# Moving a hybrid layer's SBUF buffers by 64 and 128 bytes

## The chip, the cores and the metric

The kernel runs on one core of a Trainium2 chip. The metric is the time of one execution on the device, in microseconds (us). All data are float32 in HBM; the result is float32.

## What is computed

One decoder layer over 256 tokens with 2048 features. The input is normed and goes through one combined projection of 12304 columns; its parts feed a gated DeltaNet branch (8 heads of 128, short convolution, delta rule) and a causal attention branch (8 heads of 128). Each branch is widened to 2048, the two are merged with sigmoid gates, projected once more, normed and added to the input:

```python
h = rms_norm(x, pre_norm_w)                     # x: 256 x 2048
proj = h @ w_in                                 # w_in: 2048 x 12304
qkv = silu(causal_depthwise_conv(proj[:, :3072], conv_w))
oa = gated_delta_rule(l2_normalize(q), l2_normalize(k), v, beta, g)
oa = oa * rsqrt(mean(oa * oa) + eps) * gdn_norm_w * silu(gdn_z)
u_a = oa @ w_branch_a                           # 1024 x 2048
ob = moba_attention(q_b, k_b, v_b) * silu(moba_z)
u_b = ob @ w_branch_b                           # 1024 x 2048
merged = sigmoid(gate_a) * u_a + sigmoid(gate_b) * u_b
out = x + rms_norm(merged @ w_out, post_norm_w) # w_out: 2048 x 2048
```

With 256 tokens there is one attention block, so the attention is plain causal attention.

## The kernel before

**Split weights.** Every float32 weight tile is taken apart in `split` (L260): `hi` is the weight rounded to float32r (a copy on ScalarE, L265), `lo` the rest (a subtraction on VectorE, L266). The input and the branch results are held the same way, as a rounded half and a rest. A product is three float32r matmuls: rounded by hi, rounded by lo, rest by hi. All of them are recorded by the helper `mm` (L176), transposes by `tr` (L179), in the order in which the program names them.

**Projections.** `proj_n` (L419) makes a chunk of 512 output columns: for each of 16 slices of 128 features it loads rows of w_in into a raw tile (pool `wraw`, three buffers, on the SyncE queue, L424), splits it in two (pool `wspl`, three buffers of hi and lo), and runs 12 matmuls per split: two slices, two halves of the tokens, three products. The moving operand is hi or lo with 512 columns (348, 348 and 344 for the three chunks of zg), the stationary one a 128 by 128 piece of the normed input, tile hT. A chunk of 512 columns is 96 matmuls. In `proj_t` (L397: the DeltaNet's q and k) it is the other way round: the weight is stationary and hT moves, with 512 and 256 columns.

**The normed input.** hT is an object of class `Halves` (L63) over two tiles, hT_0 for slices 0 to 7 and hT_1 for slices 8 to 15, so that the first half of a chunk's matmuls reads the one and the second half the other.

**Branches and output.** `seven` (L990) multiplies blocks of the branch and output weights with seven block products in place of eight (names ua, ub, y). Some operands are sums of blocks: of the weights in tiles z0, z1, z2, and of the input in four pairs of tiles, three of them in tt, tw, tv of the pool `big` and the fourth in tag s of the pool `wk` (`sum_tiles`). `product` (L964) runs 6 or 12 matmuls for a split. While the branch blocks run, chunks of the gates ga and gb run beside them (`gate_beside`, L1066).

**Every fourth split.** When the first branch block begins, `branch_pair` (L1031) closes the pool `wf` and opens a pool `wx` with one buffer in its room; from then on every fourth split takes its hi and lo from `wx` and the others from `wspl` (L262).

**Where buffers lie.** Tiles lie in SBUF pool by pool: cst, big, wraw, wspl, wk, then wf or wx; within a pool in the order of first allocation, at steps of 32 bytes per partition. Most tiles are multiples of 256 bytes per partition long. Counted from a multiple of 256 bytes, the tiles of big, wraw and wspl lie at 0, the s tiles of wk at 64, wf and wx at 192.

**Two small rows.** nrow (L193) holds the norm's weight as 16 rows of 128, loaded on the ScalarE queue and read by a transpose at the start. grs (L485, in `decays`) holds the decays of the DeltaNet, 16 rows of 128, copied from PSUM and written to DRAM at once by the GpSimd queue (L488). Each has a place of 512 bytes in cst.

Of the kernel before, what the change touches and what calls it, by code (L numbers as in the profile page):

```python
# [8 lines left out]
F32 = mybir.dt.float32  # L9
F32R = mybir.dt.float32r  # L10
# [5 lines left out]
P = 128  # L16
EPS = 1e-6
NEG = -1e30

WARM = 2  # L20
WARM2 = 1
# [84 lines left out]
def hybrid_layer(  # L106
# [16 lines left out]
    B, S, D = x.shape  # L123
    NT = S // P
    KT = D // P
# [16 lines left out]

    cst = ctx.enter_context(tc.tile_pool(name="cst", bufs=1))
    big = ctx.enter_context(tc.tile_pool(name="big", bufs=1))
    wraw = ctx.enter_context(tc.tile_pool(name="wraw", bufs=3))
    wspl = ctx.enter_context(tc.tile_pool(name="wspl", bufs=3))
    wk = ctx.enter_context(tc.tile_pool(name="wk", bufs=2))
    dram = ctx.enter_context(tc.tile_pool(name="dram", bufs=1, space=bass.MemoryType.DRAM))

    early = ExitStack()  # L150
    wf = early.enter_context(tc.tile_pool(name="wf", bufs=8))
    acc = ctx.enter_context(tc.tile_pool(name="acc", bufs=4, space=bass.MemoryType.PSUM))
# [5 lines left out]
    def aux_tile(name):  # L158
        return aux.tile([P, 512], F32, tag="aux", name=name)
# [15 lines left out]
    def mm(*args, **kwargs):  # L175
        return pin(nc.tensor.matmul(*args, **kwargs))  # L176

    def tr(*args):
        return pin(nc.tensor.transpose(*args))  # L179
# [4 lines left out]
    nba = 2 * H  # L184
# [1 line left out]
    ZG = (0, 348, 696, GW + nba)  # L186
    ZW, ZBA = ZG[3] - ZG[2], GW - ZG[2]

    nrow = cst.tile([KT, P], F32, name="nrow")
    rawk = [big.tile([P, KT // 2, 512], F32, tag=f"g{i}", name=f"rawf_k{i}") for i in range(2)]  # L190
    ones = cst.tile([P, P], F32, name="ones")
    nc.vector.memset(ones, 1.0)
# [14 lines left out]
    for c in range(KT // 2):  # L207
# [24 lines left out]
    nc.gpsimd.affine_select(  # L232
        out=mask_t, in_=mask_t, compare_op=ALU.is_ge, fill=NEG, base=0, pattern=[[1, P]], channel_multiplier=-1
    )
# [10 lines left out]
        compare_op=ALU.is_ge,  # L245
        fill=NEG,
        base=0,
# [19 lines left out]
        return hi, lo  # L267

    ncol = cst.tile([P, KT], F32, name="ncol")
    hT = Halves(*(big.tile([P, KT // 2, 2 * S], F32R, tag=f"hT{i}", name=f"hT_{i}") for i in range(2)))  # L270
    ssx = cst.tile([P, NT, 4], F32, name="ssx")

    def turn(c):
# [176 lines left out]
    def decays():  # L450

        pbt = [pt[:, ZBA:ZW] for pt in pzg]
        zz = cst.tile([P, NT, H], F32, name="zz")
        sp = cst.tile([P, NT, H], F32, name="sp")
        for t in range(NT):
            pa_ = pbt[t][:, H:]
            pin(nc.vector.scalar_tensor_tensor(zz[:, t, :], pa_, rstd[:, t : t + 1], dtb, op0=ALU.mult, op1=ALU.add))
        for t in range(NT):
            pb_ = pbt[t][:, :H]
            pin(nc.scalar.activation(beta[:, t, :], pb_, AF.Exp, scale=nrstd[:, t : t + 1]))  # L460
        pin(nc.scalar.activation(sp, zz, AF.Abs))
        pin(nc.scalar.activation(sp, sp, AF.Exp, scale=-1.0))
        pin(nc.scalar.activation(na, na, AF.Exp))
        pin(nc.scalar.activation(sp, sp, AF.Ln, bias=ones[:, 0:1]))
        pin(nc.vector.scalar_tensor_tensor(sp, zz, 0.0, sp, op0=ALU.max, op1=ALU.add))
        pin(
            nc.vector.scalar_tensor_tensor(
                sp, sp, -1.0, na.unsqueeze(1).to_broadcast([P, NT, H]), op0=ALU.mult, op1=ALU.mult
            )
        )  # L470
        nc.vector.tensor_scalar_add(beta, beta, 1.0)
        nc.vector.reciprocal(beta, beta)
        yield 0.5
        for f in late:
            f()
        yield PG_WAIT
        pg = aux_tile("pg")
        mm(pg[:, 0:nba], tri_u, sp, start=True, stop=True)
        mm(pg[:, nba : nba + H], ones, sp[:, 0, :], start=True, stop=True)
        nc.vector.tensor_copy(gcol, pg[:, 0:nba].rearrange("p (t h) -> p t h", t=NT))  # L480
        nc.vector.tensor_tensor(gx, pg[:, nba : nba + H], gcol[:, 0, :], op=ALU.subtract)
        yield PGT_WAIT
        pgt = aux_tile("pgt")
        tr(pgt[0:nba, :P], gcol.rearrange("p t h -> p (t h)"), ident)
        grs = cst.tile([nba, P], F32, name="grs")  # L485
        nc.vector.tensor_copy(grs, pgt[0:nba, :P])
        g_d = dram.tile([nba, P], F32, name="g_d")
        nc.gpsimd.dma_start(g_d, grs)  # L488
        grow = big.tile([P, NT, H, P], F32, tag="z0", name="grow")
        nc.gpsimd.dma_start(  # L490
            grow.rearrange("p t h n -> p (t h n)"),
            g_d.rearrange("a n -> (a n)").unsqueeze(0).broadcast_to([P, nba * P]),
        )
        yield D_WAIT
        for h in range(0, H, 2):
            for h_ in (h, h + 1):
                for t in range(NT):
                    pin(
                        nc.vector.scalar_tensor_tensor(
                            dec[:, h_, 2 * t * P : (2 * t + 1) * P],  # L500
                            grow[:, t, h_, :],
                            gcol[:, t, h_ : h_ + 1],
                            mask_t,
                            op0=ALU.subtract,
                            op1=ALU.add,
                        )
                    )
            pin(
                nc.vector.tensor_tensor(
                    dec[:, h : h + 2, P : 2 * P],  # L510
                    grow[:, 1, h : h + 2, :],
                    gx[:, h : h + 2].unsqueeze(2).to_broadcast([P, 2, P]),
                    op=ALU.add,
                )
            )
            yield 1


        one = wk.tile([P, 2], F32, tag="mx", name="one")
        pin(nc.vector.memset(one, 1.0))  # L520
        identity.append(big.tile([P, 16, 64], F32, tag="tv", name="tv"))
        for g in range(4):
            gp = slice(32 * g, 32 * g + 32)
            nc.gpsimd.affine_select(
                out=identity[0][gp],
                in_=one[gp, 0:1].unsqueeze(2).to_broadcast([32, 16, 64]),
                compare_op=ALU.is_equal,
                fill=0.0,
                base=g,
                pattern=[[4, 16], [-1, 64]],  # L530
                channel_multiplier=0,
            )
        for h in range(0, H, 2):
            pin(nc.scalar.activation(dec[:, h : h + 2, :], dec[:, h : h + 2, :], AF.Exp))
            if h + 2 < H:
                yield 1
        decaying.pop()
# [877 lines left out]
    pzg = proj_n(w_in, CZ + ZG[2], hT, KT, "zg2", ZW, aux_tile)  # L1415
    late.append(lambda: silu_out("zg", ZG[2], GW, pzg))
    gq.add(decays())
    for m in range(4):
        conv_silu(kTs[m // 2][m % 2], H + m, late)
# [306 lines left out]
```

## Time and profile before

| | us |
|---|---|
| median of 3 runs | 747.8 |
| lowest and highest | 747.5, 748.63 |
| span of the profiled execution | 745.7 |
| TensorE busy (matmuls) | 736.9 |
| VectorE busy | 606.8 |
| ScalarE busy | 456.2 |
| GpSimd busy | 90.8 |
| HBM traffic | 187.49 MB, mean 251 GB/s |

The span goes from the first to the last instruction of one execution; the time of a run also holds what lies around them. PE stands for TensorE's matmuls, PEld for its weight loads, DVE for VectorE, ACT for ScalarE, POOL for GpSimd, SP for SyncE. Matmuls are pipelined: the next one starts while the one before still drains, so that a matmul's duration is longer than the time from its start to the next one's start.

### The profile page before, as it was taken

To read this page: it belongs to the slowest core of one execution; us is meant where nothing else is said; L and a number is where in the kernel's file an instruction comes from. 1 tells how busy PE (TensorE), PEld (TensorE's weight loads), DVE (VectorE), ACT (ScalarE), POOL (GpSimd) and SP (SyncE) were. 2 spreads that over 40 slices of the span, in tenths; PEclk is the share of its full clock that TensorE was granted. 3 is DMA by queue.
4 is the path that set the end of the run, shared out by engine and by line. 5 is a ranking of instruction groups with operands and counts; after the bars stand their busy time and mean duration, and the time that the engine had idled before them with its cause. 6 is when DMAs were issued, how large, how long until landed. Compare 5 with 4: busy or idle time off the path is not lost.

```text
span 745.7 us, 9927 instructions
## 1 busy us (share of the span) xinstructions
PE 736.9 (99%) x3594; PEld 621.2 (83%) x3594; DVE 606.8 (81%) x957; ACT 456.2 (61%) x692; POOL 90.8 (12%) x124
## 2 busy tenths in 40 slices
PE   9999999999999999999999999999999999999995
PEld 7898988898888888888888888788888888888885
DVE  6877779997896998987556889688796799988864
ACT  6777655556775665547556766557546654765751
POOL 1000301113110101232011050010000101110000
PEclk9999999999999999999999999999999999999999
DMA  9576586548766767998478799788988889998862
GB/s 317 177 242 227 164 237 203 173 143 271 258 226 226 254 215 260 302 303 300 140 228 307 256 294 307 209 320 244 352 228 301 236 300 276 383 328 228 270 238 113
DMA packets 94199, 187.49 MB, mean 251 GB/s; under 512 B 4421, under 2 KB 25606, under 8 KB 93638
## 3 DMA queue, kind: packets, MB, share of 16 engines
q1 hardware_dynamic: 76806, 134.83, 53.9%
q0 software_dynamic: 15584, 47.20, 21.9%
q10 hardware_dynamic: 1760, 4.83, 1.8%
q8 instruction: 28, 0.46, 0.2%
q14 instruction: 21, 0.17, 0.1%
HBM read 173.20 MB, written 13.64 MB: 251 GB/s over the span
## 4 chain that ended last, share of the span: by engine, by line
PE 98%; DMA 0%; DVE 0%; DVEq 0%; issue 0%; ACTq 0%; ACT 0%
PE a_ga L176 12%; PE a_gb L176 12%; PE a_y L176 9%; PE a_ub L176 7%; PE a_zg L176 6%; PE a_k L176 6%; PE a_q L176 6%; PE a_mq L176 6%; PE a_mv L176 6%; PE a_mk L176 6%; PE a_v L176 6%; PE a_zm L176 6%; PE a_ua L176 5%; PE s L176 1%; PE po L176 1%; PE so L176 1%
## 5 line engine op out<-in xcount | busy, mean ns | idle before, releaser
L176 PE MATMUL a_ga<-hi_ga,hT 128*128 128x512 f32 x256 | 81.7, 393 | 0.0
L176 PE MATMUL a_gb<-hi_gb,hT 128*128 128x512 f32 x256 | 80.9, 391 | 0.0
L176 PEld LDWEIGHTS a_gb<-hi_gb,hT 128*128 128x128 f32 x256 | 48.0, 188 | 10.6
L176 PEld LDWEIGHTS a_ga<-hi_ga,hT 128*128 128x128 f32 x256 | 48.1, 188 | 10.1
L265 ACT CAST hi_gb<-raw_gb 128x1024 fp32r<-128x1024 f32 x32 | 33.5, 1052 | 28.1 <-PE a_gb L176 15.2
L266 DVE TENSOR_TENSOR lo_ga<-raw_ga,hi_ga 128x1024 fp32r<-128x1024 f32 x32 | 38.9, 1218 | 14.3 <-ACT hi_ga L265 14.1
L176 PE MATMUL a_ga<-lo_ga,hT 128*128 128x512 f32 x128 | 50.0, 391 | 0.0
L176 PE MATMUL a_gb<-lo_gb,hT 128*128 128x512 f32 x128 | 50.0, 391 | 0.0
L176 PE MATMUL a_zg<-hi_zg,hT 128*128 128x348 f32 (+1 forms) x192 | 46.7, 322 | 0.0
L265 ACT CAST hi_ga<-raw_ga 128x1024 fp32r<-128x1024 f32 x32 | 33.4, 1049 | 20.4 <-PE a_ga L176 16.8
L266 DVE TENSOR_TENSOR lo_gb<-raw_gb,hi_gb 128x1024 fp32r<-128x1024 f32 x32 | 38.7, 1216 | 7.3 <-ACT hi_gb L265 7.0
L176 PE MATMUL a_mv<-hi_mv,hT 128*128 128x512 f32 x128 | 41.5, 395 | 0.0
L176 PE MATMUL a_mk<-hi_mk,hT 128*128 128x512 f32 x128 | 40.5, 393 | 0.0
L176 PE MATMUL a_q<-hT,hi_q 128*128 128x512 f32 x128 | 40.2, 395 | 0.0
L176 PE MATMUL a_mq<-hi_mq,hT 128*128 128x512 f32 x128 | 39.7, 389 | 0.0
L176 PE MATMUL a_v<-hi_v,hT 128*128 128x512 f32 x128 | 39.7, 389 | 0.0
L176 PE MATMUL a_zm<-hi_zm,hT 128*128 128x512 f32 x128 | 39.7, 389 | 0.0
L176 PE MATMUL a_k<-hT,hi_k 128*128 128x512 f32 (+1 forms) x129 | 38.2, 397 | 0.0
L176 PEld LDWEIGHTS a_zg<-hi_zg,hT 128*128 128x128 f32 x192 | 33.5, 188 | 0.1
L266 DVE TENSOR_TENSOR lo_mv<-raw_mv,hi_mv 128x1024 fp32r<-128x1024 f32 x16 | 19.4, 1218 | 17.2 <-ACT hi_mv L265 16.0
L176 PE MATMUL a_zg<-lo_zg,hT 128*128 128x348 f32 (+1 forms) x96 | 30.9, 322 | 0.0
L265 ACT CAST hi_zg<-raw_zg 128x696 fp32r<-128x696 f32 (+1 forms) x24 | 18.5, 771 | 19.7 <-PE a_zg L176 7.4
(479 smaller groups left out, 2025.2 us busy)
## 6 DMA issues: line engine op xcount, KB each, us to landing
raw_ga<-in_w_in_dram SPq DMA_DIRECT2D x16, 1024.0 KB, 6.0
raw_gb<-in_w_in_dram SPq DMA_DIRECT2D x16, 1024.0 KB, 7.0
raw_y<-in_w_out_dram SPq DMA_DIRECT2D x14, 1024.0 KB, 7.8
raw_q<-in_w_in_dram SPq DMA_DIRECT2D x8, 1024.0 KB, 5.5
raw_mv<-in_w_in_dram SPq DMA_DIRECT2D x8, 1024.0 KB, 5.0
raw_v<-in_w_in_dram SPq DMA_DIRECT2D x8, 1024.0 KB, 5.0
raw_zm<-in_w_in_dram SPq DMA_DIRECT2D x8, 1024.0 KB, 5.2
raw_mq<-in_w_in_dram SPq DMA_DIRECT2D x8, 1024.0 KB, 6.4
```

The lines of the kernel that those rows point to most:

```text
L176: return pin(nc.tensor.matmul(*args, **kwargs))
L265: nc.scalar.copy(hi, raw)
L266: nc.vector.tensor_tensor(lo, raw, hi.bitcast(F32), op=ALU.subtract)
```

## The change

Three small tiles that nothing reads or writes are added. pad_w (16 floats, 64 bytes per partition) lies in front of wraw, pad_h (64 bytes) between hT_0 and hT_1, and pad_x (64 bytes) in front of the pool wf, in whose room wx is opened later. nrow and grs share one place (tag rows), which takes 512 bytes out of cst. Counted from a multiple of 256 bytes: hT_0 and the tiles allocated with it (g0, g1, ga, u1) stay at 0; hT_1 and what is allocated behind it (z0, z1, z2, tv, tt, tw) lie at 64; wraw and wspl at 128; the s tiles of wk at 192; wf and wx at 128. The instructions stay the same.

```diff
--- before.py
+++ after.py
@@ -16,6 +16,8 @@
 P = 128
 EPS = 1e-6
 NEG = -1e30
+
+PAD_H, PAD_W, PAD_X = 16, 16, 16
 
 WARM = 2
 WARM2 = 1
@@ -142,11 +144,13 @@
 
     cst = ctx.enter_context(tc.tile_pool(name="cst", bufs=1))
     big = ctx.enter_context(tc.tile_pool(name="big", bufs=1))
+    ctx.enter_context(tc.tile_pool(name="pad_w", bufs=1)).tile([P, PAD_W], F32, name="pad_w")
     wraw = ctx.enter_context(tc.tile_pool(name="wraw", bufs=3))
     wspl = ctx.enter_context(tc.tile_pool(name="wspl", bufs=3))
     wk = ctx.enter_context(tc.tile_pool(name="wk", bufs=2))
     dram = ctx.enter_context(tc.tile_pool(name="dram", bufs=1, space=bass.MemoryType.DRAM))
 
+    ctx.enter_context(tc.tile_pool(name="pad_x", bufs=1)).tile([P, PAD_X], F32, name="pad_x")
     early = ExitStack()
     wf = early.enter_context(tc.tile_pool(name="wf", bufs=8))
     acc = ctx.enter_context(tc.tile_pool(name="acc", bufs=4, space=bass.MemoryType.PSUM))
@@ -186,7 +190,7 @@
     ZG = (0, 348, 696, GW + nba)
     ZW, ZBA = ZG[3] - ZG[2], GW - ZG[2]
 
-    nrow = cst.tile([KT, P], F32, name="nrow")
+    nrow = cst.tile([KT, P], F32, tag="rows", name="nrow")
     rawk = [big.tile([P, KT // 2, 512], F32, tag=f"g{i}", name=f"rawf_k{i}") for i in range(2)]
     ones = cst.tile([P, P], F32, name="ones")
     nc.vector.memset(ones, 1.0)
@@ -267,7 +271,9 @@
         return hi, lo
 
     ncol = cst.tile([P, KT], F32, name="ncol")
-    hT = Halves(*(big.tile([P, KT // 2, 2 * S], F32R, tag=f"hT{i}", name=f"hT_{i}") for i in range(2)))
+    hT0 = big.tile([P, KT // 2, 2 * S], F32R, tag="hT0", name="hT_0")
+    big.tile([P, PAD_H], F32, name="pad_h")
+    hT = Halves(hT0, big.tile([P, KT // 2, 2 * S], F32R, tag="hT1", name="hT_1"))
     ssx = cst.tile([P, NT, 4], F32, name="ssx")
 
     def turn(c):
@@ -482,7 +488,7 @@
         yield PGT_WAIT
         pgt = aux_tile("pgt")
         tr(pgt[0:nba, :P], gcol.rearrange("p t h -> p (t h)"), ident)
-        grs = cst.tile([nba, P], F32, name="grs")
+        grs = cst.tile([nba, P], F32, tag="rows", name="grs")
         nc.vector.tensor_copy(grs, pgt[0:nba, :P])
         g_d = dram.tile([nba, P], F32, name="g_d")
         nc.gpsimd.dma_start(g_d, grs)
```

## Rows read from the trace of the kernel before

**Rows 1.** The page: span, busy time and share of each engine.

```profile
span 745.7 us, 9927 instructions
PE 736.9 (99%) x3594; PEld 621.2 (83%) x3594; DVE 606.8 (81%) x957; ACT 456.2 (61%) x692; POOL 90.8 (12%) x124
```

**Rows 2.** The page, part 4: the chain that ended last, by engine.

```profile
PE 98%; DMA 0%; DVE 0%; DVEq 0%; issue 0%; ACTq 0%; ACT 0%
```

**Rows 3.** The chain in order of time: start us, length us, engine and tile.

```profile
110.39 11.15 PE a_k L176 x64
...
176.57 21.80 PE a_v L176 x96
198.37 21.76 PE a_zm L176 x96
...
547.45 21.96 PE a_gb L176 x96
```

**Rows 4.** Windows: us; PE, PEld, DVE, ACT, POOL busy; PEclk; DMA; GB/s.

```profile
176.50:198.30 21.80, 21.80 (x98) 18.02 (x97) 15.00 (x27) 15.75 (x31) 5.07 (x8) 1.00 0.83 262
...
621.70:643.60 21.90, 21.90 (x98) 17.94 (x97) 21.90 (x28) 12.21 (x15) 2.79 (x3) 1.00 1.03 316
```

**Rows 5.** Timeline of PE in gb: start us, us, operation (out<-moving,stationary).

```profile
552.98 0.39 PE L176 MATMUL a_gb<-lo_gb,hT 128*128 128x512 f32 x1
...
555.70 0.39 PE L176 MATMUL a_gb<-lo_gb,hT 128*128 128x512 f32 x1
...
558.49 0.40 PE L176 MATMUL a_gb<-lo_gb,hT 128*128 128x512 f32 x1
...
561.24 0.39 PE L176 MATMUL a_gb<-lo_gb,hT 128*128 128x512 f32 x1
```

**Rows 6.** Timeline of PE around the fourth sums of ua.

```profile
494.97 0.39 PE L176 MATMUL a_ua<-hi_ua0p,oas_hi 128*128 128x512 f32 x1
...
497.77 0.40 PE L176 MATMUL a_ga<-hi_ga,hT 128*128 128x512 f32 x1
...
536.27 0.40 PE L176 MATMUL a_ua<-hi_ua2p,oas_hi 128*128 128x512 f32 x1
...
537.67 0.39 PE L176 MATMUL a_ua<-hi_ua2p,oas_hi 128*128 128x512 f32 x1
...
539.05 0.39 PE L176 MATMUL a_gb<-hi_gb,hT 128*128 128x512 f32 x1
```

**Rows 7.** Timeline of PE in zg, with 344 and 348 columns.

```profile
38.78 0.32 PE L176 MATMUL a_zg<-lo_zg,hT 128*128 128x344 f32 x1
...
39.73 0.32 PE L176 MATMUL a_zg<-lo_zg,hT 128*128 128x344 f32 x1
...
40.68 0.32 PE L176 MATMUL a_zg<-lo_zg,hT 128*128 128x344 f32 x1
...
85.62 0.32 PE L176 MATMUL a_zg<-lo_zg,hT 128*128 128x348 f32 x1
...
86.58 0.32 PE L176 MATMUL a_zg<-lo_zg,hT 128*128 128x348 f32 x1
...
87.54 0.32 PE L176 MATMUL a_zg<-lo_zg,hT 128*128 128x348 f32 x1
```

**Rows 8.** DMA issues: KB each, median us from issue to landing.

```profile
raw_v<-in_w_in_dram SPq DMA_DIRECT2D x8, 1024.0 KB, 5.0
...
raw_zg<-in_w_in_dram SPq DMA_DIRECT2D x8, 696.0 KB, 4.3
```

**Rows 9.** Tiles nrow and grs: min/median/max ns, first and last start us.

```profile
L179 PE MATMUL pnc<-ident,nrow x1: 256/256/256, 4.2 to 4.2; 16*128 16x16 f32 x1
...
L486 DVE COPY grs<-pgt x1: 273/273/273, 64.1 to 64.1; 16x128 f32<-16x128 f32 x1
```

## The prediction, made before the change was run

> **What bounds the kernel now.** I read the page first. Its span is 745.7 us and the matmul engine is busy in 99% of it, VectorE in 81%, ScalarE in 61% [rows 1]; the chain of work that ended last is 98% TensorE [rows 2]. So the kernel is as long as its matmul stream, and a change that only moves buffers can act on the time in two ways: through the time from one matmul's start to the next one's (below: the pitch), or through something off the stream that gets late enough to stop it. The profiled execution spans 745.7 us and the runs have a median of 747.8: 2.1 us lie around the first and the last instruction, and I add them back unchanged.
>
> The chain in order of time gives the pitch: 96 matmuls of 512 columns for zm in 21.76 us are 226.7 ns each; v has 227.1; a gb chunk of the later part has 21.96 us, 228.8 each [rows 3]. 512 columns at 2.4 GHz (granted clock 1.00, the upper level, [rows 4]) are 213.3 ns, so each matmul pays 13.4 ns, or 6%, on top of its columns. That margin is what the change can touch. The mean duration in the lists of groups (389 to 397 ns) is no help: matmuls overlap, and only starts count.
>
> **Where the addresses show already.** The change speaks of places modulo 256 bytes, and the kernel before holds several of them, so the trace prices some. From the sizes of the tiles, wspl, hT and nearly all of "big" start at 0; wx, which takes every fourth split after the first branch block, at 192; the s tiles of wk (the fourth sum of each seven-product block) at 64. I write a pair as (moving, stationary).
> - (0, 0) and (192, 0): in gb the lo matmuls that open three splits in a row stand at 552.98, 555.70, 558.49 and 561.24 [rows 5]. Twelve matmuls from wspl take 2.72 us (226.7 each), the twelve from wx 2.79 (232.5 with the edge matmul), the next twelve from wspl 2.75. So a wx split costs some 6.6 ns more per matmul, and the stream needs about 0.02 to 0.03 us to find its pace again.
> - (0, 64): twelve matmuls on the fourth sum take 2.80 us, 233.3 each; a second such block six in 1.40 [rows 6].
> - (192, 64), 128 apart: the six behind it take 1.38 us, 230 each [rows 6].
> - 348 and 344 columns: in zg the second k of each split begins 1392 or 1376 bytes later, at 112 or 96. Six matmuls at 0 and six at 112 both take 0.96 us; six at 0 and six at 96 both 0.95 [rows 7].
>
> The settled paces are 160.0, 226.7 and 233.3 ns: 24, 34 and 35 times 6.67 ns. A relation therefore costs a whole step or nothing, once the stream has settled; values between (230) stand only in short stretches.
>
> **The change part by part.** PAD_H moves hT's second half and all of "big" allotted behind it (z0 to z2, tv, tt, tw) to 64; PAD_W with it puts wraw and wspl at 128; PAD_X puts wx at 128 as well. No instruction is added or removed. (a) *Matmuls with split weights as moving operand.* The 18 chunks of v, zm, mq, mk, mv, ga, gb have 96 each, 1728; by the code the seven-product blocks and the rest of ua, ub and y have about 684. Some 1308 of these become (128, 0), some 1044 (128, 64), and 60 (the fourth sums) (128, 192). No row has either of the first two. Bounds from the nearest rows: 233.3, the price of (192, 0) and (0, 64), so +6.6 ns; below, one step less than now, 220.0, since nothing in the rows excludes a gain and 213.3 would still fit under it. I take 226.7, because the rows nearest to 128 are 96 and 112, they are long and regular, and they cost what 0 costs; the row that is 128 apart (230) has six matmuls, right behind a disturbance. (b) *wx.* 32 splits go through it, 15 with 12 matmuls and 17 with six: 282. At 226.7 each saves 6.6 ns, 1.9 us, and the 32 recoveries at 0.02 us save 0.6. Sum of (a) and (b): -2.5 us; bounds of (b) alone: -2.5 and 0. (c) *The fourth sums* keep their distance (0 to 64 becomes 128 to 192): 60 matmuls, 0, with 60 x 6.7 = 0.4 us either way. (d) *q and k*: hT is the moving operand there, 64 matmuls with 24,576 columns take 11.15 us [rows 3], 14.2 ns above the columns each. They become (0, 128) and (64, 128); about 510 matmuls by 3 ns either way are 1.5 us; I take 0. (e) *zg's 288*: bounded by a step of 6.7 ns on each either way, 1.9 us; I take 0. (f) *Loads into moved places.* raw_zg lands rows of 1392 bytes at odd places: 696 KB in 4.3 us against 1024 KB in 5.0 for raw_v [rows 8], a rate 21% lower at worst. wraw has three buffers of 5.4 us of matmuls each, so a load of 7 us that became 9 would still land inside the two buffers ahead of it; I take 0, and the cover is thin only where the DMA engines are full (rival 4). (g) *The shared row.* grs is written at 64.1 us and waits from now on for the last reader of nrow, which ran at 4.2 us [rows 9]: nothing is queued by it, cost 0.
>
> Sum: 745.7 - 2.5 + 2.1 = 745.3 us.
>
> **A rule against it.** The rows show that the same matmul with the same data sizes takes 226.7 or 233.3 ns with only the buffer's place changed [rows 5]. The Trainium skill, "SBUF — State Buffer", section "SBUF: two separate sides", holds that on the engine side only the port pair shared by VectorE and GpSimd contends and that TensorE waits for no one; by it the places of buffers could not matter and the time would stay 747.8. The trace disagrees with it, by those 6.6 ns. The page "TensorE: Matmul & The Clock Gate" of the Trainium skill, section "Wait — 56ns, not 53.3ns?", puts a warm pitch at the columns plus 2.5 ns, 215.8; this trace has nowhere such a pitch on 512 columns, and an estimate from that page's figure, 2352 x 10.9 ns, would be 26 us off.
>
> **The rivals.** (1) *The new relations cost a step or half of one*: slower. For: both long stretches away from (0, 0) pay it [rows 5, 6], and the one 128 apart pays half. Against: 96 and 112 pay nothing [rows 7]. Price: half a step (3.3 ns) on 2070 matmuls is +6.8, less 0.9 for wx and 0.6 for recoveries: 753.1. One of the two halves at a full step: between 752 and 754 as well. Both halves: 2070 x 6.67 = +13.8, 761.6. It decides as soon as more than some 380 of the matmuls pay a step. (2) *The new relations save a step* (220.0 ns): for one of the halves -7.0 or -8.7 besides the 2.5, about 737; for both -15.7 - 1.9 - 0.6, 729.6. Against: no pace under 226.7 is in the trace, and in the gb chunk of 621.7 VectorE is busy in all of the stretch and the DMA engines too [rows 4], so part of the gain would be given back there as waits for lo or raw. (3) *Places do not matter as such*, and what I read as places belongs to the order of buffers: 747.8. Against: 32 splits of wx alike, and the s tiles in other products. (4) *Loads get slower*: if rows at 64 or 128 cost 5% where DMA is full (the last 200 us), 2% to 4% of these show, 752 to 756.
>
> **How the numbers follow.** My forecast (places cost as now, wx gains): 0.34, 743.8 to 747.5 on its own. Rival 1: 0.33. Rival 2: 0.20. Rival 3: 0.08. Rival 4: 0.05. A measurement of this kernel can tell about 0.2%, 1.5 us, from no change. Faster takes 0.30 of the forecast and all of rival 2; within 0.2% takes 0.04 of the forecast and rival 3; slower the rest. Cases of both signs hold most of the chance, so the range of 8 in 10 runs from 732 (one half saving a step, or most of both) to 758 (more than one half paying one); outside lie the full gain and the full loss.
>
> **What would show it.** Right: zm's chunk still 21.76 us, gb's chunk 21.8 in place of 21.96, and no difference between every fourth split and the others. Rival 1 shows as 22.1 to 22.4 us for zm, in one half of the chunk or in both (the halves are the first and last 48 matmuls); rival 2 as 21.1; rival 4 as waits of TensorE for hi or raw with an unchanged pitch. The forecast is wrong if 128 or 64 bytes do not lie on the same flat as 96 and 112.

## The result, and the profile after

The changed kernel takes 754.0 us (median of 4 runs, 753.82 to 756.01) against 747.7 before: 1.009 times the time before, 95% interval 1.0076 to 1.0104. It is slower by 6.3 us; the forecast was 745.3, faster. The range of 732 to 758 holds 754.0, but only because it held cases of both signs.

The page of the kernel after, first its span and the busy time of each engine, then the chain that ended last by engine:

```profile
span 752.3 us, 9927 instructions
PE 743.5 (99%) x3594; PEld 621.6 (83%) x3594; DVE 607.1 (81%) x957; ACT 456.5 (61%) x692; POOL 90.5 (12%) x124
...
PE 99%; DVE 0%; ACT 0%; DVEq 0%; issue 0%
```

The same number of instructions, the same busy time within 0.4 us on every other engine, and 6.6 us more on TensorE, which is also what the span grew by [rows 1, 2]. Nothing new waits. So the loss is in the time from one matmul's start to the next one's, the pitch. The clock is not the cause: in the chunk of v the granted clock is 1.00, the upper level, with the DMA engines busy for 0.84 of the time, as in the same chunk before (1.00 and 0.83 [rows 4]). Window of the kernel after (us; PE, PEld, DVE, ACT, POOL busy; PEclk; DMA; GB/s):

```profile
176.60:198.74 22.14, 22.14 (x98) 18.07 (x97) 15.29 (x27) 15.84 (x31) 5.06 (x8) 1.00 0.84 259
```

The chain in order of time of the kernel after (start us, length us, engine and tile, count):

```profile
110.44 11.13 PE a_k L180 x64
...
176.60 22.13 PE a_v L180 x96
198.74 22.16 PE a_zm L180 x96
...
512.95 5.60 PE a_gb L180 x24
...
524.05 5.60 PE a_gb L180 x24
...
535.19 5.49 PE a_gb L180 x24
...
543.48 5.59 PE a_gb L180 x24
...
551.87 22.19 PE a_gb L180 x96
```

A chunk of v, zm or gb is 0.2 to 0.4 us longer than before, the group of k is 0.02 us shorter [rows 3]. Timeline of PE in the chunk of zm after (start us, us, operation), with three of its matmuls that have lo as moving operand; every third matmul is one:

```profile
198.81 0.40 PE L180 MATMUL a_zm<-lo_zm,hT 128*128 128x512 f32 x1
...
209.97 0.39 PE L180 MATMUL a_zm<-lo_zm,hT 128*128 128x512 f32 x1
...
219.58 0.39 PE L180 MATMUL a_zm<-lo_zm,hT 128*128 128x512 f32 x1
```

From the first to the second are the 48 matmuls on hT_0: 11.16 us, 232.5 ns each. From the second to the third are 42 on hT_1: 9.61 us, 228.8 each. Before, it was 226.7 in both halves. Worked out from all start times of the two traces and the places that the program gives the tiles (pitches over 275 ns, which hold waits, left out, and for fewer columns those as far above the time of the columns; a pair is moving, stationary):

| matmuls | before | after | change |
|---|---|---|---|
| 512 columns, wspl, first half | (0,0) 227.5 ns | (128,0) 232.7 | 1112 x 5.2 = +5.8 us |
| 512 columns, wspl, second half | (0,0) 227.3 | (128,64) 229.4 | 918 x 2.1 = +1.9 |
| 512 columns, wx, first half | (192,0) 233.3 | (128,0) 232.9 | 150 x -0.4 = -0.1 |
| 512 columns, wx, second half | (192,0) 233.3 | (128,64) 229.9 | 120 x -3.4 = -0.4 |
| fourth sums | (0,64) 233.2 | (128,192) 233.3 | 0 |
| zg, 344 and 348 columns | 159.0 | 158.3 | 288 x -0.7 = -0.2 |
| q and k, 512 and 256 columns | 174.6 | 174.4 | 510 x -0.2 = -0.1 |

Sum: +6.9 us, against 6.6 in the span.

### The profile page after: what moved, and what is told of

Its sections match the earlier page's. It is cut to its first block, busy times and chain, and to the rows that moved or that the text cites. A ratio compares the mean times of both kernels' runs of the same rounds, so it can differ in the third digit from the quotient of the medians.

```text
span 752.3 us, 9927 instructions
## 1 busy us (share of the span) xinstructions
PE 743.5 (99%) x3594; PEld 621.6 (83%) x3594; DVE 607.1 (81%) x957; ACT 456.5 (61%) x692; POOL 90.5 (12%) x124
## 4 chain that ended last, share of the span: by engine, by line
PE 99%; DVE 0%; ACT 0%; DVEq 0%; issue 0%
PE a_gb L180 12%; PE a_ga L180 12%; PE a_y L180 9%; PE a_ub L180 7%; PE a_k L180 6%; PE a_zg L180 6%; PE a_mv L180 6%; PE a_q L180 6%; PE a_mq L180 6%; PE a_mk L180 6%; PE a_zm L180 6%; PE a_v L180 6%; PE a_ua L180 5%; PE s L180 1%; PE po L180 1%; PE so L180 1%
```

## The experiments

Theory 1: the pair of places sets the pitch, by the prices above. Its rivals: the distance of the two places alone (theory 2), the load of the SBUF by DMA and the other engines (theory 3), slower loads into moved places.

**The grid of places.** The layer is replaced by cells of 36 matmuls, each cell with its own pair of places:

```python
mh, ml = hi[:, r % 2, m // 4 : m // 4 + w], lo[:, r % 2, m // 4 : m // 4 + w]
for t in range(2):
    sh = st[:, k, s // 4 + 128 * t : s // 4 + 128 * t + 128]
    sl = st[:, k, s // 4 + 256 + 128 * t : s // 4 + 256 + 128 * t + 128]
    matmul(pts[t][:, :w], sh, mh); matmul(pts[t][:, :w], sh, ml); matmul(pts[t][:, :w], sl, mh)
```

> This kernel leaves the layer out. It holds 64 cells, each 36 float32r matmuls of 512 columns in the order of a chunk (rounded by hi, rounded by lo, rest by hi, for two halves of the tokens), with the moving operand at one of eight places modulo 256 (0 to 224 in steps of 32) and the stationary one at one of eight; nothing else runs beside them. Every cell comes twice, in two orders. Theory 1 (the pair of places sets the pitch): the cells repeat what the traces of the two kernels show, (0,0) 227 ns, (192,0) and (0,64) 233, (128,0) 232.5, (128,64) 229.5, and both visits of a cell agree within 1 ns. Theory 2 (only the distance of the two places counts): all cells of one distance are alike, so (64,64) and (128,128) take 227 as (0,0) does. Theory 3 (not the places but the load of the SBUF by the other engines and the DMA): all cells take the same, 227 or less.

Timeline of PE in the grid: for each of five cells two starts that are 12 matmuls apart. In order: (0,0), (0,64), (64,64), (128,0), (128,128):

```profile
14.38 0.39 PE L45 MATMUL a<-hi,st 128*128 128x512 f32 x1
...
17.10 0.39 PE L45 MATMUL a<-hi,st 128*128 128x512 f32 x1
...
31.02 0.40 PE L45 MATMUL a<-hi,st 128*128 128x512 f32 x1
...
33.82 0.40 PE L45 MATMUL a<-hi,st 128*128 128x512 f32 x1
...
164.62 0.39 PE L45 MATMUL a<-hi,st 128*128 128x512 f32 x1
...
167.34 0.39 PE L45 MATMUL a<-hi,st 128*128 128x512 f32 x1
...
281.64 0.40 PE L45 MATMUL a<-hi,st 128*128 128x512 f32 x1
...
284.44 0.39 PE L45 MATMUL a<-hi,st 128*128 128x512 f32 x1
...
314.98 0.39 PE L45 MATMUL a<-hi,st 128*128 128x512 f32 x1
...
317.70 0.39 PE L45 MATMUL a<-hi,st 128*128 128x512 f32 x1
```

2.72 us where the two places are equal, be it 0, 64 or 128, and 2.80 at (0,64) and (128,0). All 128 visits by distance (moving minus stationary place, modulo 256; mean pitch behind the first 12 matmuls of a visit, 16 visits of eight cells each):

| distance | 0 | 32 | 64 | 96 | 128 | 160 | 192 | 224 |
|---|---|---|---|---|---|---|---|---|
| mean ns | 226.7 | 233.3 | 228.8 | 233.2 | 232.7 | 234.2 | 233.4 | 233.3 |
| lowest | 226.7 | 233.3 | 228.7 | 233.1 | 232.3 | 234.1 | 233.3 | 233.3 |
| highest | 226.7 | 233.3 | 229.0 | 233.5 | 232.8 | 234.3 | 233.5 | 233.4 |

Theory 2 holds, and theory 1 with it, since a pair fixes its distance: the cells of a distance agree within 0.5 ns, whatever the two places are. The changed kernel's halves have the distances 128 and 64, and their pitches are the grid's (232.7 and 228.8). Theory 3 falls, since the pitches are there while no other engine works and the granted clock is 1.00; the page of the grid, over its whole span:

```profile
DMA packets 612, 4.78 MB, mean 4 GB/s; under 512 B 64, under 2 KB 64, under 8 KB 64
```

What may lie behind the distance shows in the timeline of PE and its weight loads (PEld) in the grid:

```profile
299.97 0.39 PE L46 MATMUL a<-lo,st 128*128 128x512 f32 x1
299.97 0.19 PEld L47 LDWEIGHTS a<-hi,st 128*128 128x128 f32 x1
300.20 0.39 PE L47 MATMUL a<-hi,st 128*128 128x512 f32 x1
```

The weights of the next matmul (line 47) are loaded for 0.19 us from the moment at which the matmul of line 46 begins to stream its columns. Both read the SBUF at once; that the distance counts for this reason is not shown by it.

**wx at 0 alone.** The kernel before with the pad in front of wf and no other:

```diff
-PAD_H, PAD_W, PAD_X = 16, 16, 16
+PAD_H, PAD_W, PAD_X = 0, 0, 16
...
```

> The kernel before with a pad of 64 bytes in front of the pool wf alone (and the shared row): wx lies at 0, everything else as before. Theory 1 (pairs of places, prices of the two traces): 270 matmuls of wx fall from 233.3 to 227.4, so 1.6 us less than before: 746.1. Theory 3 (the load of other engines sets the pitch, wx is slow because it has one buffer): 747.7, as before.

Measured: 745.33 us, 0.9973 of before (0.9963 to 0.9983). The kernel before took 747.39 in the runs beside it. Chain of this kernel:

```profile
198.40 21.76 PE a_zm L179 x96
...
547.71 21.76 PE a_gb L179 x96
```

Timeline of PE in that chunk of gb, four starts with 12 matmuls from each to the next:

```profile
551.85 0.39 PE L179 MATMUL a_gb<-lo_gb,hT 128*128 128x512 f32 x1
...
554.57 0.39 PE L179 MATMUL a_gb<-lo_gb,hT 128*128 128x512 f32 x1
...
557.29 0.39 PE L179 MATMUL a_gb<-lo_gb,hT 128*128 128x512 f32 x1
...
560.01 0.39 PE L179 MATMUL a_gb<-lo_gb,hT 128*128 128x512 f32 x1
```

2.72 three times: every fourth split is as fast as the others now, where it took 2.79 before [rows 5], and gb is at 21.76 in place of 21.96 [rows 3]. The 2.1 us gained are step (b) of the prediction (2.5) by itself; the expectation of 1.6 had left the recoveries out.

**The two halves of the change apart.** First the weights at 128 and the whole input at 0, then the weights at 0 and hT_1 at 64:

```diff
-PAD_H, PAD_W, PAD_X = 16, 16, 16
+PAD_H, PAD_W, PAD_X = 0, 32, 16
...
-    big.tile([P, PAD_H], F32, name="pad_h")
```

> The changed kernel without the pad inside the input: hT and all of big at 0, wraw, wspl and wx at 128. Theory 1: every matmul with split weights is (128,0), 232.7 in place of 227.4 on about 2050 of them, 10.9 us more than before: 758.4, slower than the changed kernel, whose second half had (128,64). Rival (the second half is cheap for another reason than the place of hT_1): 754, as the changed kernel. Rival (the loss is in the loads into moved places): 754 too, with an unchanged pitch.

```diff
-PAD_H, PAD_W, PAD_X = 16, 16, 16
+PAD_H, PAD_W, PAD_X = 16, 48, 16
```

> The changed kernel with the weights put back: hT_1 and what is allocated behind it at 64, wraw, wspl and wx at 0. Theory 1: the first half of each chunk is (0,0) at 227.4, the second (0,64) at 233.2 on some 920 matmuls, 5.3 us more; wx gains 0.9 in its first half: 752.2. Rival (64 for the second half is good by itself, as it looks in the changed kernel, where that half is the cheaper one): 746 or less.

Measured: 757.07 us (1.0128 of before, 1.0113 to 1.0144) and 751.55 (1.0054, 1.0042 to 1.0067). Chain of the first:

```profile
199.19 22.31 PE a_zm L180 x96
...
554.40 22.31 PE a_gb L180 x96
```

And of the second:

```profile
198.77 22.11 PE a_zm L180 x96
...
551.25 22.08 PE a_gb L180 x96
```

22.31 us are 232.4 ns for all 96 matmuls: without the pad inside the input the second half pays as the first, and the kernel is slower still. 22.11 are 230.3, the mean of 227 and 233.4: with the weights at 0 the same pad costs, since it turns the second half's distance from 0 into 192. So 64 bytes under hT_1 are neither good nor bad by themselves, as theories 1 and 2 have it and the rival did not.

**Finer distances, and whose weights.** As the grid, with distances in steps of 4 bytes, and with two pairs in turn:

```python
for a, o in ((hi, 0), (lo, 0), (hi, 256)):
    m, s = places[j % len(places)]
    j += 1
    f = s // 4 + o + 128 * t
    matmul(pts[t][:, :w], st[:, k, f : f + 128], a[:, r % 2, m // 4 : m // 4 + w])
```

> This kernel leaves the layer out and measures the pitch of 512-column matmuls alone, as the grid of places did, now with distances (moving minus stationary place) from -32 to 96 bytes in steps of 4, and 128, 256, 512, 768 and 1024; and cells in which two pairs of places alternate from one matmul to the next. Theory A (the distance modulo 256 counts, on a grid of 32 bytes or finer): 256, 512, 768 and 1024 take 226.7 as 0 does, and between 0 and 32 the pitch goes from 226.6 to 233.4 at one point or in steps; a distance that takes 220 is possible at a place that the grid of 32 left out, I give it one chance in five. Theory B (the distance modulo 512 or more): 256 takes 230 or more. For the alternating pairs: if a matmul is slowed by the load of the weights of the next one while its own columns stream, then (0,0),(128,128) is slow (232.8) and (0,128),(128,0) fast (226.7); if its own pair counts, the other way round.

Timeline of PE, two starts that are 12 matmuls apart in each of three cells: distance 4; the pairs (0,128),(128,0) in turn; the pairs (0,0),(128,128) in turn:

```profile
79.81 0.40 PE L49 MATMUL a<-lo,st 128*128 128x512 f32 x1
...
82.64 0.40 PE L49 MATMUL a<-lo,st 128*128 128x512 f32 x1
...
182.65 0.39 PE L49 MATMUL a<-lo,st 128*128 128x512 f32 x1
...
185.41 0.39 PE L49 MATMUL a<-lo,st 128*128 128x512 f32 x1
...
296.70 0.40 PE L49 MATMUL a<-lo,st 128*128 128x512 f32 x1
...
299.54 0.40 PE L49 MATMUL a<-lo,st 128*128 128x512 f32 x1
```

Four bytes cost 10 ns (236.7). Distances of 256, 512, 768 and 1024 take 226.7, so 256 bytes are the period; 226.7 came also at -4, 28 and 60, up to 240 at -12, 20 and 68, and nothing below 226.7 anywhere: the chance of one in five that I gave to 220 did not come true. The pairs in turn: with each matmul's own pair equal and the next weights 128 away, 2.84 us, 236.7 ns; the other way round 2.76, 230.0. That fits next weights that count for more than the matmul's own, as the overlap in the timeline suggests. It is not settled: the second one is not down at 226.7, and the first is above the 232.7 of a cell in which both are 128 away, so the two do not simply add up.

**Other widths.** The same loop with the stationary operand at 0 and other numbers of columns:

> As the grid of places, the layer left out: the stationary operand at 0, the moving one at places 0 to 240, with 256, 320, 344, 348, 384, 448, 480 and 496 columns. Theory A (the start of the moving operand counts): place 0 is the fastest at every width. Theory B (what counts is the place that the stream of columns has reached when the next weights are loaded, so the width comes in too): the fastest place shifts with the width; it is 0 at 256, 320, 384 and 448 columns (whole multiples of 256 bytes) and lies elsewhere at 344, 348, 480 and 496, and at 344 and 348 the places 0, 96 and 112 are all slow or all middling, which is why the rows with 344 and 348 columns before the change showed no difference.

Timeline of PE, cells with 348 columns and the moving operand at 144, at 112 and at 0, two starts 12 matmuls apart in each:

```profile
136.10 0.32 PE L49 MATMUL a<-lo,st 128*128 128x348 f32 x1
...
137.94 0.32 PE L49 MATMUL a<-lo,st 128*128 128x348 f32 x1
...
194.62 0.32 PE L49 MATMUL a<-lo,st 128*128 128x348 f32 x1
...
196.54 0.32 PE L49 MATMUL a<-lo,st 128*128 128x348 f32 x1
...
356.92 0.32 PE L49 MATMUL a<-lo,st 128*128 128x348 f32 x1
...
358.82 0.32 PE L49 MATMUL a<-lo,st 128*128 128x348 f32 x1
```

153.3 ns at 144, 160.0 at 112, 158.3 at 0. With 348 columns the good place is 144 (16 came to the same pace on one of its two visits), and 0 and 112 are both bad. With 512 columns 0 is good. The place that is cheapest moves with the width, as theory B says, but not by the rule that it gave: at 256 columns 0 and 96 are the dearest (120.0), and 192 has the cheapest visit (113.3) but 117.8 on its other one; at 448, 64 and 160 (200.0) beat 0 (202.7); at 320 all eight places take 146.7. At 344 columns no place has 153.3 on both visits: 0 and 112 settled there once and at 157.7 and 159.8 the other time, and 96 took 157.5.

**q and k.** The same with two matmuls of 512 columns on hi and two of 256 on lo:

> As the grid of places, the layer left out, in the order of q and k: two matmuls of 512 columns with hi stationary, two of 256 with lo; the moving operand at 0, hi at eight places and lo at eight. Both kernels have 174.5 ns a matmul at (0,0) and about 174 at 128. If the distance of the next weights counts, hi and lo matter apart; the best cell has about 173.3 (160 for the columns and 13.3), the worst 180.

With hi and lo both at 0, as in the kernel before, 174.2 ns a matmul; the cheapest of the 64 cells have 172.9 (both at 192) and 173.1 to 173.4 (five others), the dearest 178.6; the first cell of the run, whose matmuls still took 427 ns at its start, is left out. On 510 matmuls the best is worth about 0.7 us. It was not tried in the layer.

**Loads alone, and everything together.** Both are the kernel with wx at 0 and one thing more. First the raw tiles at 128 with all that TensorE reads at 0:

```diff
+    ctx.enter_context(tc.tile_pool(name="pad_r", bufs=1)).tile([P, 32], F32, name="pad_r")
     wraw = ctx.enter_context(tc.tile_pool(name="wraw", bufs=3))
+    ctx.enter_context(tc.tile_pool(name="pad_s", bufs=1)).tile([P, 32], F32, name="pad_s")
     wspl = ctx.enter_context(tc.tile_pool(name="wspl", bufs=3))
```

> As the kernel with wx at 0, but the raw tiles wraw at 128 with everything else at 0: loads, ScalarE and VectorE see the moved place, TensorE sees none. Theory: 745.4, as with wx alone. Rival (part of the loss of the changed kernel is in loads into moved places, which land 0.3 us later there): 746.5 or more.

Then the weights at 128 as in the changed kernel, and the input and the branch results there too:

```diff
+    ctx.enter_context(tc.tile_pool(name="pad_b", bufs=1)).tile([P, 32], F32, name="pad_b")
     big = ctx.enter_context(tc.tile_pool(name="big", bufs=1))
```

> As the kernel with wx at 0, but big, wraw, wspl, wk, wf and wx all moved by 128 bytes: the weights lie where the changed kernel has them, and the input and the branch results move along, so every distance is as in the kernel with wx at 0. Theory (distance): 745.4. Rival (a place of its own costs, 128 for the weights): 752 to 757.

Measured: 745.54 us (0.9975, 0.9964 to 0.9986) and 745.68 (0.9978, 0.9969 to 0.9987): both as with wx alone. Of the first the DMA issue of raw_v (KB, median us to landing):

```profile
raw_v<-in_w_in_dram SPq DMA_DIRECT2D x8, 1024.0 KB, 5.1
```

The same from the kernel after:

```profile
raw_v<-in_w_in_dram SPq DMA_DIRECT2D x8, 1024.0 KB, 5.4
```

And from the kernel with the weights at 128 and the whole input at 0, the slowest of all:

```profile
raw_v<-in_w_in_dram SPq DMA_DIRECT2D x8, 1024.0 KB, 5.0
```

The loads landed 0.4 us later in the changed kernel, 0.1 with wraw moved alone, and no later than before [rows 8] in the kernel that lost most, where wraw lies at 128 as well. So the loss does not follow the landing; why the changed kernel's loads landed later stays open. From the chain of the kernel in which everything lies at 128:

```profile
200.08 21.76 PE a_zm L180 x96
```

Weights at 128 with an input at 128 have the 21.76 us of before. With the weights in the same place, the changed kernel needs 22.16; what it lost is the price of the distance to the input.

**The priced distances put right.** The kernel with wx at 0, with the s tiles of wk at 0 and the split weights of zg in rows of 384:

```diff
+PAD_H, PAD_W, PAD_X = 0, 0, 32
+ZSHIFT = {348: 36, 344: 0}
+    ctx.enter_context(tc.tile_pool(name="pad_k", bufs=1)).tile([P, 48], F32, name="pad_k")
...
+        if shape[-1] in ZSHIFT:
+            o = ZSHIFT[shape[-1]]
+            hi, lo = (
+                pool.tile([P, 2 * 384 + o], F32R, tag=g, name=f"{g}_{name}")[:, o:].rearrange("p (k c) -> p k c", k=2)[
+                    :, :, : shape[-1]
+                ]
+                for g in ("hi", "lo")
+            )
...
```

> The kernel before with wx at 0, the s tiles of wk at 0, and the split weights of zg in rows of 384 in place of 348 or 344 floats: both rows of a 348-column split at 144, those of the 344-column one at 0. Theory (the distance between the streaming operand and the next weights sets the pitch, at each width its own): 1.6 to 2.1 us from wx as measured with wx alone, 0.3 to 0.4 us from the 60 fourth-sum matmuls (233.3 to 226.7), 192 matmuls of 348 columns from 159.6 to 153.3 are 1.2 us, 96 of 344 from 157.7 to 155.5 are 0.2: 743.8, against 747.5. Rival (the paces of the bare grid do not hold beside loads and other engines): 745.4, as with wx alone.

Measured: 743.88 us, 0.9946 of before (0.9932 to 0.996), which took 747.44 in the runs beside it. It is the fastest of all. Its chain, and then the timeline of PE in that chunk of zg, three starts with 12 matmuls from each to the next:

```profile
81.88 14.76 PE a_zg L181 x96
```

```profile
83.30 0.32 PE L181 MATMUL a_zg<-lo_zg,hT 128*128 128x348 f32 x1
...
85.14 0.32 PE L181 MATMUL a_zg<-lo_zg,hT 128*128 128x348 f32 x1
...
86.98 0.32 PE L181 MATMUL a_zg<-lo_zg,hT 128*128 128x348 f32 x1
```

12 matmuls take 1.84 us, 153.3 each, where two times six took 1.92 before [rows 7]: the grid's price for 144 holds in the full kernel. The price for 344 columns does not: they take 157.8 with both rows at 0, worked out from all their starts, where 155.5 was expected. That figure was the mean of the two visits of a cell that settled at 157.7 and at 153.3.

## Why the prediction was wrong, step by step

- **What bounds the kernel** was right: the stream of matmuls was the path before and after, and all of the 6.6 us came through the pitch.
- **(a) the split weights** failed, and with it the sign. The step was "I take 226.7, because the rows nearest to 128 are 96 and 112, they are long and regular, and they cost what 0 costs". Those rows have 344 and 348 columns. At 348 columns both 0 and 112 are dear (158.3 and 160.0, against 153.3 at 144), and at 344 columns the places 0 and 96 lie close too (157.7, on a second visit 153.3, against 157.5), so that no difference between them meant no cheap place among them, not a flat on which all places are cheap. The row with 512 columns that was 128 apart showed 230 [rows 6], and I set it aside as six matmuls behind a disturbance; it was the nearer row. Measured, in place of 226.7 and 0: 232.7 ns and +5.8 us for (128, 0), 229.4 ns and +1.9 us for (128, 64).
- **"A relation costs a whole step or nothing"** failed too. Distance 64 settles in a repeating 226, 229, 232 ns (mean 228.8), which is a third of the step, in the grid as in the changed kernel; distance 128 repeats patterns with a mean of 232 to 233.5.
- **The pair** was the right notion for part of the way. I wrote it as (moving, stationary) but argued with each place's own distance from a multiple of 256 ("one flat"). What counts is the difference of the two.
- **(b) wx** was right for what it was: 2.1 us measured when wx alone went to 0, 2.5 forecast. In the change it went to 128, where it gains 0.5; this hung on (a).
- **(c), (d), (e)** were taken at 0 and came to 0, -0.1 and -0.2 us. **(f)** was right: no loss from loads into moved places shows in the time. **(g)** was right; grs is written at 64.0 us in place of 64.1.
- **Rival 1** is what happened, with 0.33 given to it against 0.34 for the forecast, and its sum came close: 753.1 for half a step (3.3 ns) on 2070 matmuls, 754.0 measured, 5.2 ns in one half and 2.1 in the other. It counted 1.5 us of gain from wx, of which 0.5 came. **Rival 3** (places do not matter) falls by the grid: with nothing else at work the place of a buffer moves the pitch from 226.7 to 234.2. So what the prediction drew from the Trainium skill, "SBUF — State Buffer", section "SBUF: two separate sides", falls too, namely that places cannot matter because TensorE waits for no one. The sentence itself is not refuted by that: in the grid no other engine was there to wait for.

What stays open: which part of the SBUF or of TensorE's read path makes the distance count, why a width shifts the cheap place as it does, how the matmul's own weights and the next ones share in it (230.0 and 236.7 with the pairs in turn), and on which of its paces a stream settles where two visits differ.

## What to carry to other kernels

When the stream of matmuls is the path, look at the starts in the timeline, not at durations: a pitch that differs between buffers of the same shape is a price of their places, and padding by some bytes gets it back. What counts is the distance between the operand that streams and the weights (in these kernels a matmul's own weights and those loaded meanwhile lie at the same place), so an edit that moves the one must be checked against the other; for float32r matmuls of 512 columns no distance was cheaper than equal places modulo 256 bytes, and for another width the price has to be measured at that width, on more than one visit. A row of another shape is not a near row, even if its place is near.

## What was not expected of the hardware

- TensorE's pitch at 512 columns depends on the distance of two SBUF places at a resolution of 4 bytes and with a period of 256: 226.7 ns at 0, 236.7 at 4, 233.3 at 32, with nothing else running.
- The pace has a memory. In the chain of the kernel after, the third and the fourth group of 24 for gb (535.19 and 543.48) run the same pair (128,64), and take 5.49 and 5.59 us: the second one comes behind a block at (128,192) and keeps its 233.3 ns to the end. Some finer distances, too, settled differently on their two visits (distance -8: 233.4 and 230.1), and so did some places at other widths (344 columns at 0: 157.7 and 153.3). In the first grid all visits of a distance agree within 0.5 ns.
- The cheapest place differs with the number of columns: 0 for 512, 144 for 348, 64 and 160 for 448, the same on both visits of each.
